# One PSUM operand in the vector operations of norms, reciprocal roots and activations of a two-layer diffusion backbone

## The chip, the cores and the metric

The kernel runs on one core of a Trainium2 chip, as one launch. The metric is the device time of the core in microseconds. The engines that matter are TensorE (PE, with its weight loads as PEld), VectorE (DVE), ScalarE (ACT), GpSimd (POOL) and SyncE (SP), which issues most DMAs. PSUM is the memory that TensorE writes its results to, eight banks of 512 float32 columns on 128 partitions; SBUF is the larger memory that holds everything else.

## What is computed

The reference runs two layers over 512 latent tokens (stream X) and 256 context tokens (stream C) with 1024 features. Each layer is a half-step SwiGLU feed-forward network (FFN), a token mixer (layer 0: gated convolution and Fourier mixing; layer 1: differential and latent attention) and a second FFN. Each of these parts has a norm ahead of it and a norm behind it:

```python
def rmsnorm(x, g):
    x32 = x.astype(jnp.float32)
    y = x32 * lax.rsqrt(jnp.mean(x32 * x32, axis=-1, keepdims=True) + EPS)
    return (y * g.astype(jnp.float32)).astype(x.dtype)

def modulate(h, g, shift, scale):
    return rmsnorm(h, g) * (1 + scale) + shift

def swiglu(x, w_in, w_out):
    gate, up = jnp.split(x @ w_in, 2, axis=-1)
    return (jax.nn.silu(gate) * up) @ w_out

def macaron_ffn(h, m, g, w_in, w_out, slot):
    xm = modulate(h, g[2 * slot], m[:, :, 3 * slot], m[:, :, 3 * slot + 1])
    y = swiglu(xm, w_in, w_out)
    return h + FFN_RES * m[:, :, 3 * slot + 2] * rmsnorm(y, g[2 * slot + 1])
```

The shift, scale and gate vectors `m` come from the conditioning vectors (adaLN), a product that the kernel computes on VectorE. The last norms have only X to serve, which the kernel then handles as two halves of 256 tokens, A and B.

## The kernel before

**Layout.** Features lie on partitions, tokens on columns: a stream is eight tiles `h[k]` of 128 x 512 (X) or 128 x 256 (C, A, B). Products are made to float32 accuracy in three matmuls (`mm3`, L213 to L215): each operand is split into a rounded high part and a low remainder, and high x high, high x low and low x high are added in PSUM. Weights come by SP's DMAs into `wraw`, ScalarE copies the high part `wh` (L141), and the low part `wl` is a subtraction on POOL or VectorE in turn (L142, L143). While a norm is under way (`self.norms`), all of these subtractions go to POOL.

**PSUM.** Three rings share the eight banks: `mm` has three slots of one bank, `st` one slot of one bank, `pr` two slots of two banks. The matmuls of C, and of the output projections of both streams, go to `mm`; gate and up of X to `pr`; norm statistics to `st`.

**A norm.** While the last block of an output projection runs, each finished tile is added to `y` (L486), ScalarE squares it (L235) and VectorE adds the square to `ssum` (L236). When all eight are done, PE multiplies `ssum` with ones into `st` (L249), VectorE computes the reciprocal root with some twelve operations of two or four columns (`rsqrt`, L264 to L275: a first guess by integer arithmetic and three Newton steps), and PE spreads it over the partitions (L255). Then `post` runs for each tile k: `t = y * A * rb` (L315), `h += t` (L317), square, add to `ssum`. A second L249, root and L255 follow, and `pre` makes the input of the next part: `t = h * A * rb` (L294), its high part on ScalarE (L300), its low part on VectorE (L301); for tile 0 of X, the low part is made by POOL (L298). `activated` (L413, with `split`) forms silu(gate) x up and its two parts.

**What sets the order.** One program is written out in Python; its jobs are interleaved by a clock of estimated microseconds (`advance`, `yield`), and a list scheduler then fixes the order on each engine, with a higher priority for the norms. On the chip each engine runs its own list in order. X's norm is placed beside the last gate, up and output projection of C; C's norm beside the first gate and up matmuls of X's next part. Stream X is lane `x`, C lane `c`; A and B are lanes `x` and `c`. In the first FFN, X starts with `lead6`: three pairs of gate and up at once, two of them in `pr`, the third in two `mm` slots.

Of the kernel before, what the change touches and what calls it, by code (L numbers as in the profile page):

```python
# [10 lines left out]
F32 = mybir.dt.float32  # L11
# [3 lines left out]
AF = mybir.ActivationFunctionType  # L15
ALU = mybir.AluOpType
AX = mybir.AxisListType

P = 128
# [3 lines left out]
CTX = 256  # L23
FT = 2816 // P
EPS = 1e-6
# [1 line left out]
POST = (1.8, 1.1)  # L27
N1 = 3.0
N2 = 4.0
POOL_LO = (0,)  # L30
LEAD = 2
TBUFS = 3
TABUFS = 2
# [43 lines left out]
class Builder:  # L77
# [146 lines left out]
    class Stats:  # L224
        pass

    def stats_add(self, s, st, src):

        nc = self.nc
        if st.ssum is None:  # L230
            st.ssum = self.tmp.tile([P, s.n], F32, name=self.nm("ssum"), tag=f"ssum{s.lane}", bufs=1)
            nc.scalar.activation(out=st.ssum, in_=src, func=AF.Square)
        else:
            sq = self.t(s.n)
            nc.scalar.activation(out=sq, in_=src, func=AF.Square)  # L235
            nc.vector.tensor_tensor(out=st.ssum, in0=st.ssum, in1=sq, op=ALU.add)  # L236

# [5 lines left out]
    def rnorm(self, s, st, width):  # L243

        nc = self.nc
        with self.tc.high_priority(PRIORITY):
            cp = self.bank()
            for b in range(s.nb):
                nc.tensor.matmul(cp[:, b:b + 1], st.ssum[:, b * P:(b + 1) * P], self.ones, start=True, stop=True)  # L249
            r = self.rsqrt(cp[:, :s.nb], 1.0 / width)  # L250
        yield N2
        with self.tc.high_priority(PRIORITY):
            bc = self.bank()
            for b in range(s.nb):
                nc.tensor.matmul(bc[:, b * P:(b + 1) * P], r[:, b:b + 1].to_broadcast([P, P]), self.ident,  # L255
                                 start=True, stop=True)
        self.clock += s.nb * 0.213
        return bc[:, :s.n]

    def rsqrt(self, src, scale, eps=EPS):  # L260

        v, n = self.nc.vector, src.shape[-1]
        r, t, m = (self.tmp.tile([P, 8], F32, name=self.nm("rs"), tag="rs", bufs=6)[:, :n] for _ in range(3))
        if isinstance(eps, float):  # L264
            v.tensor_scalar(out=m, in0=src, scalar1=scale, scalar2=eps, op0=ALU.mult, op1=ALU.add)
        else:
            v.scalar_tensor_tensor(out=m, in0=src, scalar=scale, in1=eps, op0=ALU.mult, op1=ALU.add)
        v.tensor_scalar(out=r.bitcast(I32), in0=m.bitcast(I32), scalar1=-0.5, scalar2=float(0x5F3759DF),
                        op0=ALU.mult, op1=ALU.add)
        v.tensor_scalar(out=m, in0=m, scalar1=-0.5, scalar2=None, op0=ALU.mult)  # L270
        for _ in range(3):
            v.tensor_tensor(out=t, in0=r, in1=r, op=ALU.mult)
            v.tensor_tensor(out=t, in0=t, in1=m, op=ALU.mult)  # L273
            v.scalar_tensor_tensor(out=r, in0=t, scalar=1.5, in1=r, op0=ALU.add, op1=ALU.mult)
        return r  # L275

# [13 lines left out]
    def pre_tile(self, s, k, A, B, rb):  # L290
        nc = self.nc
        x = self.xmpool.tile([P, 2, s.n], F32R, name=self.nm("xm"), tag=f"xm{s.name}{k}", bufs=1)
        t = self.t(s.n)
        nc.vector.scalar_tensor_tensor(out=t, in0=s.h[k], scalar=A[:, k:k + 1], in1=rb, op0=ALU.mult, op1=ALU.mult)  # L294
        if s.n == 512 and k in POOL_LO:
            nc.scalar.activation(out=t, in_=t, func=AF.Identity, bias=B[:, k:k + 1])
            nc.scalar.activation(out=x[:, 0], in_=t, func=AF.Copy)
            nc.gpsimd.tensor_tensor(out=x[:, 1], in0=t, in1=x[:, 0].bitcast(F32), op=ALU.subtract)  # L298
        else:
            nc.scalar.activation(out=x[:, 0], in_=t, func=AF.Identity, bias=B[:, k:k + 1])  # L300
            nc.vector.scalar_tensor_tensor(out=x[:, 1], in0=t, scalar=B[:, k:k + 1], in1=x[:, 0].bitcast(F32),  # L301
                                           op0=ALU.add, op1=ALU.subtract)
        return x[:, 0], x[:, 1]

    def post(self, s, st, A, want_stats=True):

        nc = self.nc
        y = s.y
        yield N1
        rb = yield from self.rnorm(s, st, D)  # L310
        new = self.new_stats()
        for k in range(KT):
            with self.tc.high_priority(PRIORITY):
                t = self.t(s.n)
                nc.vector.scalar_tensor_tensor(out=t, in0=y[k], scalar=A[:, k:k + 1], in1=rb,  # L315
                                               op0=ALU.mult, op1=ALU.mult)
                nc.vector.tensor_tensor(out=s.h[k], in0=s.h[k], in1=t, op=ALU.add)  # L317
                if want_stats:
                    self.stats_add(s, new, s.h[k])
            yield POST[0] if s.n == 512 else POST[1]  # L320
        yield 2.0
        return new
# [86 lines left out]
    def activated(self, s, f, g, u, acts):  # L409
        nc = self.nc  # L410
        t = self.ffpool.tile([P, s.n], F32, name=self.nm("ta"), tag="ta", bufs=TABUFS)
        nc.scalar.activation(out=t, in_=g, func=AF.Silu)
        nc.vector.tensor_tensor(out=t, in0=t, in1=u, op=ALU.mult)  # L413
        a = self.ffpool.tile([P, 2, s.n], F32R, name=self.nm("act"), tag=f"act{s.name}", bufs=5)
        self.split(t, a[:, 0], a[:, 1])
        acts[s, f] = (a[:, 0], a[:, 1])

    def lead4(self, s, ws, lead=None):
# [51 lines left out]
    def out_proj(self, s, b, c, w, acts, stats):  # L470

        nc = self.nc
        k0, nk = BLOCKS[b]
        nm = 8 // nk
        last = b == len(BLOCKS) - 1
        if b == 0 and c == 0:
            self.new_y(s)
        for i in range(nm):
            m = c * nm + i
            ps = self.mm()[:, :s.n]  # L480
            for k in range(nk):
                self.mm3(ps, self.wk(w, i * nk + k), acts[s, k0 + k], k == 0, k == nk - 1)
            if b == 0:
                nc.scalar.activation(out=s.y[m], in_=ps, func=AF.Copy)
            else:
                nc.vector.tensor_tensor(out=s.y[m], in0=s.y[m], in1=ps, op=ALU.add)  # L486
            if last:
                self.stats_add(s, stats[s], s.y[m])

    def ffn(self, l, i, s0, s1, done, ahead=0, extra=False):  # L490

# [58 lines left out]
    def mixer(self, X, C, done):  # L550
        nc, io = self.nc, self.io
# [3 lines left out]
        stats = {X: self.new_stats(), C: self.new_stats()}  # L555
# [109 lines left out]
        def out(s, m, w):  # L665
            ps = self.mm()[:, :s.n]
            order = [4, 5, 6, 7, 0, 1, 2, 3]
            for k in order:
                self.mm3(ps, self.wk(w, k), ycat[s][k], k == order[0], k == order[-1])
            nc.vector.tensor_copy(s.y[m], ps)  # L670
            self.stats_add(s, stats[s], ps)

        for step in MIX.split():
            what, s, i = step[0], {"x": X, "c": C, "b": None}[step[1]], int(step[2:] or 0)
# [149 lines left out]
    def latents(self):  # L824
# [27 lines left out]
        def keep(s, ps, lst, st):  # L852
            if lst is cq:
                tag, bufs = (("oda", 2), ("oda", 2), ("om", 1))[len(lst)]
                t = self.stg.tile([P, s.n], F32, name=self.nm("lat"), tag=tag, bufs=bufs)
            else:
                t = pool().tile([P, s.n], F32, name=self.nm("lat"), bufs=1)
            nc.scalar.activation(out=t, in_=ps, func=AF.Copy)
            self.stats_add(s, st, ps)
            lst.append(t)  # L860

        def q_lat(*ws):
# [250 lines left out]
    def da_end(self, st, g):  # L1113

        nc = self.nc
        nc.vector.scalar_tensor_tensor(out=st.den_da, in0=st.den_da, scalar=EPS, in1=st.den_da,
                                       op0=ALU.mult, op1=ALU.mult)
        rs = self.rsqrt(st.comp, 1.0 / P, st.den_da)
        for hd in range(2):
            bc = self.bank()  # L1120
            for b in range(4):
                c = hd * 4 + b
                nc.tensor.matmul(bc[:, b * P:(b + 1) * P], rs[:, c:c + 1].to_broadcast([P, P]), self.ident,
                                 start=True, stop=True)
            o = st.o_da[hd]
            nc.vector.scalar_tensor_tensor(out=o, in0=o, scalar=self.gsub, in1=bc, op0=ALU.mult, op1=ALU.mult)
            self.keep_o(g, hd, o)
# [82 lines left out]
    def attention(self, X, C, A, B, close_xm, done):  # L1210
# [34 lines left out]
        def out2(s, ms, w):  # L1245
# [6 lines left out]
            for m in ms:  # L1252
# [4 lines left out]
                    self.mm3(ps, self.wk(w, o + k), (t[:, 0, c], t[:, 1, c]), k == 0, k == len(xs) - 1)  # L1257
                o += len(xs)
                nc.vector.tensor_tensor(out=s.y[m], in0=s.y[m], in1=ps, op=ALU.add)
                self.stats_add(s, stats[s], s.y[m])  # L1260
            if ms[-1] == KT - 1:
                done(s, stats[s])

# [41 lines left out]
def body(tc, io, stop=99):  # L1305
    nc = tc.nc
    with ExitStack() as es:
# [109 lines left out]
        def begin():  # L1417
            st.update({s: b.new_stats() for s in (X, C)})
            for k in range(KT):
                b.stats_add(X, st[X], X.h[k])  # L1420
                if k == 1:
                    b.silu_late()
            norm = b.rnorm(X, st[X], D)
# [24 lines left out]
            def first():  # L1448
# [1 line left out]
                b.adaln_open(("c_ctx",))  # L1450
                load_h(C, hc, "ctx")
                for k in range(KT):
                    b.stats_add(C, st[C], C.h[k])
                    yield F2 / 8
                rb = yield from b.rnorm(C, st[C], D)
                C.xm = []
# [171 lines left out]
```

## Time and profile before

| what | value |
|---|---|
| time, median of 3 runs | 3148.69 us (3148.49 to 3149.75) |
| time of the profiled execution | 3151.14 us |
| span of the profiled execution, first to last instruction | 3149.4 us |
| mean granted clock of TensorE | 0.964 of full speed |
| ScalarE and POOL busy | 1061.5 us and 829.8 us |
| sums of squares on VectorE (L236), 172 additions | 167.4 us |
| memory read and written | 374.09 MB and 35.00 MB |

The span is cut in stretches by what runs in it: the start up to 190 us, an FFN's inner part at 190 to 560 us, the change from the first FFN to the mixer at 560 to 760 us, and so on. A group of the profile is all instructions of one line and one shape; it has their busy time, the mean length of one, and the idle time of the engine before them with what ended it. An instruction that has started but can't go on counts as busy.

### The profile page before, as it was taken

The page shows a single profiled execution, that of the slowest core. Times are in us where ns is not written, and L with a number is a line of the kernel's source. Part 1 is how long each engine was busy: PE and PEld are TensorE (multiplying, and loading weights), DVE is VectorE, ACT ScalarE, POOL GpSimd, SP SyncE. Part 2 cuts the span into 40 slices and gives each one's busy share as a digit, 9 for nine tenths or more (in the row PEclk, how much of TensorE's full clock was granted, in tenths as well). Part 3 has the DMA queues.
Part 4 walks back from the last instruction along what each step waited for, and adds up shares of the span by engine and source line. Part 5 has one row for each costly group of instructions (what it writes and reads, how often), then busy time and mean ns, then how long its engine had stood idle before and what let it go on. Part 6 is the DMA issues. An engine that isn't in the chain of part 4 may idle for free. (4 is left out here: it accounts for less than half of the span.)

```text
span 3149.4 us, 44248 instructions
## 1 busy us (share of the span) xinstructions
PE 2934.5 (93%) x17842; PEld 2605.3 (83%) x17842; DVE 1888.3 (60%) x3022; ACT 1061.5 (34%) x1744; POOL 829.8 (26%) x443
## 2 busy tenths in 40 slices
PE   6999999889979999999799999988999989899997
PEld 4878888778877988888688888876788878789997
DVE  7966666775486444445865434478366757863336
ACT  5322122334233321223431221234354546452223
POOL 4211111322242211113321111132333332442222
PEclk9999999989989999999899999989999999899998
DMA  7743334323333422232243333332876684442233
GB/s 262 237 138 127 129 120 141 107 67 122 107 119 121 135 82 99 93 108 96 79 140 114 121 116 118 114 127 96 259 186 179 156 206 96 144 154 93 96 107 122
DMA packets 189807, 412.14 MB, mean 131 GB/s; under 512 B 58337, under 2 KB 83553, under 8 KB 189602
## 3 DMA queue, kind: packets, MB, share of 16 engines
q1 hardware_dynamic: 126642, 372.05, 35.2%
q0 software_dynamic: 62960, 37.27, 5.7%
q8 instruction: 140, 2.29, 0.3%
q14 instruction: 65, 0.53, 0.1%
HBM read 374.09 MB, written 35.00 MB: 130 GB/s over the span
## 5 line engine op out<-in xcount | busy, mean ns | idle before, releaser
L143 POOL TENSOR_TENSOR wl<-wraw,wh 128x1024 fp32r<-128x1024 f32 (+1 forms) x274 | 676.9, 2473 | 2013.8 <-ACT wh L141 1992.1
L141 ACT ACTIVATE wh<-wraw 128x1024 fp32r<-128x1024 f32 (+2 forms) x474 | 491.0, 1037 | 981.2 <-PE mm L214 657.3
L213 PE MATMUL mm<-xm,wh 128*128 128x256 f32 (+1 forms) x1992 | 592.6, 298 | 10.9 <-ACT t L235 5.0
L215 PE MATMUL mm<-xm,wl 128*128 128x256 f32 (+1 forms) x1992 | 591.8, 297 | 0.3 <-DVE wl L143 0.3
L214 PE MATMUL mm<-xm,wh 128*128 128x256 f32 (+1 forms) x1992 | 591.2, 297 | 0.8 <-DVE xm L301 0.8
L214 PE MATMUL pr<-xm,wh 128*128 128x512 f32 (+1 forms) x1328 | 511.7, 385 | 7.8 <-POOL xm L1442 3.6
L213 PE MATMUL pr<-xm,wh 128*128 128x512 f32 (+1 forms) x1328 | 509.5, 385 | 7.4 <-ACT xm L300 4.0
L215 PE MATMUL pr<-xm,wl 128*128 128x512 f32 (+1 forms) x1328 | 510.7, 385 | 1.8 <-POOL wl L143 1.8
L213 PE MATMUL mm<-act,wh 128*128 128x256 f32 (+1 forms) x1408 | 464.7, 331 | 42.1 <-DVE ta L413 32.3
L214 PE MATMUL mm<-act,wh 128*128 128x256 f32 (+1 forms) x1408 | 464.4, 330 | 2.4 <-DVE act L221 2.2
L215 PE MATMUL mm<-act,wl 128*128 128x256 f32 (+1 forms) x1408 | 464.1, 330 | 0.2 <-DVE wl L143 0.2
L213 PEld LDWEIGHTS mm<-xm,wh 128*128 128x128 f32 x1992 | 381.6, 192 | 23.8 <-ACT t L235 5.4
L214 PEld LDWEIGHTS mm<-xm,wh 128*128 128x128 f32 x1992 | 381.2, 191 | 11.3 <-DVE xm L301 1.6
L215 PEld LDWEIGHTS mm<-xm,wl 128*128 128x128 f32 x1992 | 381.2, 191 | 9.7 <-DVE wl L143 0.5
L362 DVE CUSTOM_DVE_ANT_0 junk<-wmod,cond 128x1024 bf16<-128x1024 f32 x256 | 372.4, 1455 | 4.1 <-DMA wmod<-in_w_mod_dram 2.0
L143 DVE TENSOR_TENSOR wl<-wraw,wh 128x1024 fp32r<-128x1024 f32 x200 | 251.0, 1255 | 195.1 <-ACT wh L141 194.5
L213 PEld LDWEIGHTS mm<-act,wh 128*128 128x128 f32 x1408 | 272.6, 194 | 71.3 <-DVE ta L413 34.9
L214 PEld LDWEIGHTS pr<-xm,wh 128*128 128x128 f32 x1328 | 255.6, 193 | 60.9 <-POOL xm L1442 5.8
L213 PEld LDWEIGHTS pr<-xm,wh 128*128 128x128 f32 x1328 | 254.8, 192 | 58.0 <-ACT xm L300 4.4
L215 PEld LDWEIGHTS pr<-xm,wl 128*128 128x128 f32 x1328 | 255.3, 192 | 53.6 <-POOL wl L143 2.4
L214 PEld LDWEIGHTS mm<-act,wh 128*128 128x128 f32 x1408 | 273.1, 194 | 29.1 <-DVE act L221 4.8
L215 PEld LDWEIGHTS mm<-act,wl 128*128 128x128 f32 x1408 | 273.1, 194 | 25.1 <-DVE wl L143 0.7
(235 smaller groups left out, 3775.0 us busy)
## 6 DMA issues: line engine op xcount, KB each, us to landing
wraw<-in_w_ffn_in_dram SPq DMA_DIRECT2D x250, 512.0 KB, 3.5
wmod<-in_w_mod_dram SPq DMA_DIRECT2D x160, 512.0 KB, 3.8
wraw<-in_w_ffn_out_dram SPq DMA_DIRECT2D x104, 512.0 KB, 3.5
dr<-stg SPq DMA_DIRECT2D x40, 512.0 KB, 3.9
wraw<-in_w_in_even_dram SPq DMA_DIRECT2D x32, 512.0 KB, 3.5
qs<-dr POOLq DMA_DIRECT2D x56, 256.0 KB, 11.8
dr<-stg SPq DMA_DIRECT2D x36, 256.0 KB, 6.9
ks<-dr POOLq DMA_DIRECT2D x24, 384.0 KB, 11.2
```

The lines of the kernel that those rows point to most:

```text
L141: self.nc.scalar.activation(out=h, in_=r, func=AF.Copy)
L143: eng.tensor_tensor(out=l, in0=r, in1=h.bitcast(F32), op=ALU.subtract)
L213: mmul(out, w[0], x[0], start=first, stop=False)
L214: mmul(out, w[0], x[1], start=False, stop=False)
L215: mmul(out, w[1], x[0], start=False, stop=last)
L362: dot = nc.vector.tensor_tensor_reduce(out=junk, in0=w, in1=self.cond[n], op0=ALU.mult, op1=ALU.add, scale=1.0, scalar=0.0, accum_out=par[ ...
```

## The change

Each vector operation of the norms, the roots and the activations that had two operands in SBUF gets one of them in PSUM:

- The scratch tile `t` of `post` and `pre`, and the tile that receives a square, come from `scratch`: for lane `c` a slot of `mm`, for lane `x` halves of a `pr` slot. In the output projections, the mixer's output, the latents of the attention and its output projection, the square overwrites the matmul's own result tile `ps`. In the opening (`begin`, `first`), the squares go to `mm` slots.
- `rsqrt` holds `m` and `t` in columns 8 and 16 on of the `st` bank from which it reads; its Newton step multiplies r by m and then by r, where it squared r first. The attention's subnorm takes an `st` bank for it.
- `activated` multiplies in place in PSUM, and the split reads from there.
- `POOL_LO` is gone: tile 0 of X is handled like the others.

The core of the diff (the other sites of `stats_add` pass `ps`, as in `out_proj`):

```diff
-POOL_LO = (0,)
...
-    def stats_add(self, s, st, src):
+    def scratch(self, s, k, keep=False):
+
+
+        if s.lane == "c":
+            return self.mm()[:, :s.n]
+        if k == 0 or k % 2 == 0 and not keep:
+            s.scr = self.pr()
+        return s.scr[:, k % 2 * 512:k % 2 * 512 + s.n]
+
+    def stats_add(self, s, st, src, sq):
...
-            sq = self.t(s.n)
...
-            r = self.rsqrt(cp[:, :s.nb], 1.0 / width)
+            r = self.rsqrt(cp[:, :s.nb], 1.0 / width, cp)
...
-    def rsqrt(self, src, scale, eps=EPS):
+    def rsqrt(self, src, scale, bank, eps=EPS):
...
-        r, t, m = (self.tmp.tile([P, 8], F32, name=self.nm("rs"), tag="rs", bufs=6)[:, :n] for _ in range(3))
+        r = self.tmp.tile([P, 8], F32, name=self.nm("rs"), tag="rs", bufs=3)[:, :n]
+        m, t = bank[:, 8:8 + n], bank[:, 16:16 + n]
...
-            v.tensor_tensor(out=t, in0=r, in1=r, op=ALU.mult)
-            v.tensor_tensor(out=t, in0=t, in1=m, op=ALU.mult)
+            v.tensor_tensor(out=t, in0=r, in1=m, op=ALU.mult)
+            v.tensor_tensor(out=t, in0=r, in1=t, op=ALU.mult)
...
-        t = self.t(s.n)
+        t = self.scratch(s, k, True)
...
-        if s.n == 512 and k in POOL_LO:
-            nc.scalar.activation(out=t, in_=t, func=AF.Identity, bias=B[:, k:k + 1])
-            nc.scalar.activation(out=x[:, 0], in_=t, func=AF.Copy)
-            nc.gpsimd.tensor_tensor(out=x[:, 1], in0=t, in1=x[:, 0].bitcast(F32), op=ALU.subtract)
...
-                t = self.t(s.n)
+                t = self.scratch(s, k)
...
-                    self.stats_add(s, new, s.h[k])
+                    self.stats_add(s, new, s.h[k], t)
...
-        nc.vector.tensor_tensor(out=t, in0=t, in1=u, op=ALU.mult)
+        nc.vector.tensor_tensor(out=u, in0=t, in1=u, op=ALU.mult)
...
-        self.split(t, a[:, 0], a[:, 1])
+        self.split(u, a[:, 0], a[:, 1])
...
-                self.stats_add(s, stats[s], s.y[m])
+                self.stats_add(s, stats[s], s.y[m], ps)
...
-        rs = self.rsqrt(st.comp, 1.0 / P, st.den_da)
+        rs = self.rsqrt(st.comp, 1.0 / P, self.bank(), st.den_da)
...
-                b.stats_add(X, st[X], X.h[k])
+                b.stats_add(X, st[X], X.h[k], b.mm())
...
-                    b.stats_add(C, st[C], C.h[k])
+                    b.stats_add(C, st[C], C.h[k], b.mm()[:, :CTX])
```

The scheduler gives each engine nearly the same instructions (VectorE 3018 for 3016, ScalarE 1643 for 1648, POOL 440 for 444) in an order that differs at some places.

VectorE's list in X's `post` after the first FFN, before; h_109 to h_115 are tiles of X, the operations of 256 columns belong to C's activation:

```order
637 L315 SCALAR_TENSOR_TENSOR t_4907<-y_1434,par_804,st_4902 128x512
638 L315 SCALAR_TENSOR_TENSOR t_4921<-y_1435,par_804,st_4902 128x512
639 L317 TENSOR_TENSOR h_109<-h_109,t_4907 128x512
640 L317 TENSOR_TENSOR h_111<-h_111,t_4921 128x512
641 L315 SCALAR_TENSOR_TENSOR t_4945<-y_1436,par_804,st_4902 128x512
642 L236 TENSOR_TENSOR ssum_4910<-ssum_4910,t_4924 128x512
643 L317 TENSOR_TENSOR h_113<-h_113,t_4945 128x512
644 L315 SCALAR_TENSOR_TENSOR t_4988<-y_1437,par_804,st_4902 128x512
645 L236 TENSOR_TENSOR ssum_4910<-ssum_4910,t_4948 128x512
646 L413 TENSOR_TENSOR ta_4951<-ta_4951,mm_4880 128x256
```

The same place of the changed kernel, whose lines are four to seven further on (L319 was L315, L321 was L317, L243 was L236, L417 was L413):

```order
637 L319 SCALAR_TENSOR_TENSOR pr_4896<-y_1432,par_802,st_4891 128x512
638 L321 TENSOR_TENSOR h_109<-h_109,pr_4896 128x512
639 L319 SCALAR_TENSOR_TENSOR pr_4896<-y_1433,par_802,st_4891 128x512
640 L319 SCALAR_TENSOR_TENSOR pr_4932<-y_1434,par_802,st_4891 128x512
641 L321 TENSOR_TENSOR h_111<-h_111,pr_4896 128x512
642 L321 TENSOR_TENSOR h_113<-h_113,pr_4932 128x512
643 L243 TENSOR_TENSOR ssum_4899<-ssum_4899,pr_4896 128x512
644 L417 TENSOR_TENSOR mm_4869<-ta_4937,mm_4869 128x256
645 L243 TENSOR_TENSOR ssum_4899<-ssum_4899,pr_4932 128x512
646 L319 SCALAR_TENSOR_TENSOR pr_4932<-y_1435,par_802,st_4891 128x512
```

The scratch and the square now lie in two `pr` slots, the product of the activation in an `mm` slot, and C's activation stands between X's sums a little earlier.

PE's list at X's second statistics matmul (L249) in the same norm, before; act tiles of 256 columns are C's, so the matmuls around it are C's last output projection:

```order
3107 L213 MATMUL mm_5172<-act_4954,wh_5042 128x256
3109 L213 MATMUL mm_5133<-act_5118,wh_5036 128x256
3110 L213 MATMUL mm_5149<-act_5118,wh_5036 128x256
3111 L215 MATMUL mm_5172<-act_4954,wl_5043 128x256
3112 L249 MATMUL st_5182<-ones,ssum_4910 128x1 x4
3113 L213 MATMUL mm_5172<-act_5033,wh_5042 128x256
```

And in the changed kernel (L256 was L249, L212 to L214 were L213 to L215):

```order
3130 L214 MATMUL mm_5183<-act_5016,wh_5025 128x256
3131 L212 MATMUL mm_5183<-act_5096,wh_5025 128x256
3132 L213 MATMUL mm_5183<-act_5096,wh_5025 128x256
3133 L256 MATMUL st_5159<-ones,ssum_4899 128x1 x4
3134 L214 MATMUL mm_5183<-act_5096,wl_5026 128x256
3135 L212 MATMUL mm_5205<-act_4854,wh_5099 128x256
```

It stands 23 matmuls further behind in C's output projection, at its fourth tile instead of among the first three.

PE's list in the first FFN's `lead6`, at the first xm tile of X, before; wx are the weights of the third pair:

```order
13 L213 MATMUL pr_393<-xm_215,wh_314 128x512
14 L214 MATMUL pr_393<-xm_215,wh_314 128x512
15 L215 MATMUL pr_393<-xm_215,wl_315 128x512
16 L213 MATMUL mm_394<-xm_215,wx_254 128x512
17 L214 MATMUL mm_394<-xm_215,wx_254 128x512
18 L215 MATMUL mm_394<-xm_215,wx_255 128x512
```

And in the changed kernel, where xm_238 is the second tile:

```order
13 L212 MATMUL pr_392<-xm_214,wh_313 128x512
15 L212 MATMUL pr_391<-xm_238,wh_221 128x512
16 L214 MATMUL pr_392<-xm_214,wl_314 128x512
17 L213 MATMUL pr_391<-xm_238,wh_221 128x512
18 L214 MATMUL pr_391<-xm_238,wl_222 128x512
19 L212 MATMUL pr_391<-xm_238,wh_245 128x512
```

The six matmuls per tile of the third pair, 48 in all, no longer stand between the tiles: they follow behind the last of them, since the `mm` slots are given to the squares of the opening first.

More of the change, by code (lines that the diff above doesn't have):

```diff
@@ L292, in pre_tile @@
         x = self.xmpool.tile([P, 2, s.n], F32R, name=self.nm("xm"), tag=f"xm{s.name}{k}", bufs=1)
-        t = self.t(s.n)
+        t = self.scratch(s, k, True)
         nc.vector.scalar_tensor_tensor(out=t, in0=s.h[k], scalar=A[:, k:k + 1], in1=rb, op0=ALU.mult, op1=ALU.mult)
-        if s.n == 512 and k in POOL_LO:
-            nc.scalar.activation(out=t, in_=t, func=AF.Identity, bias=B[:, k:k + 1])
-            nc.scalar.activation(out=x[:, 0], in_=t, func=AF.Copy)
-            nc.gpsimd.tensor_tensor(out=x[:, 1], in0=t, in1=x[:, 0].bitcast(F32), op=ALU.subtract)
[L299 to L302, printed above, removed]
+        nc.scalar.activation(out=x[:, 0], in_=t, func=AF.Identity, bias=B[:, k:k + 1])
+        nc.vector.scalar_tensor_tensor(out=x[:, 1], in0=t, scalar=B[:, k:k + 1], in1=x[:, 0].bitcast(F32),
+                                       op0=ALU.add, op1=ALU.subtract)
         return x[:, 0], x[:, 1]
@@ L670, in out @@
             nc.vector.tensor_copy(s.y[m], ps)
-            self.stats_add(s, stats[s], ps)
+            self.stats_add(s, stats[s], ps, ps)
         for step in MIX.split():
@@ L858, in keep @@
             nc.scalar.activation(out=t, in_=ps, func=AF.Copy)
-            self.stats_add(s, st, ps)
+            self.stats_add(s, st, ps, ps)
             lst.append(t)
@@ L1259, in out2 @@
                 nc.vector.tensor_tensor(out=s.y[m], in0=s.y[m], in1=ps, op=ALU.add)
-                self.stats_add(s, stats[s], s.y[m])
+                self.stats_add(s, stats[s], s.y[m], ps)
             if ms[-1] == KT - 1:
```

## The prediction

> **What bounds the kernel now.** I read the busy shares first, then TensorE's (PE's) waits, then the span in stretches, then VectorE's (DVE's) groups by shape.
>
> ```profile
> PE 2934.5 (93%) x17842; PEld 2605.3 (83%) x17842; DVE 1888.3 (60%) x3022; ACT 1061.5 (34%) x1744; POOL 829.8 (26%) x443
> ```
>
> PE is busy for 93% of the span and nothing else comes near. So a DVE saving counts only where PE stands still for DVE. The waits of PE (microseconds in all, times, longest) name those places:
>
> ```profile
> PE st L249 <- DVE ssum L236: 43.7, 15, 7.5
> PE st L255 <- DVE rs L274: 33.4, 14, 4.3
> PE mm L213 <- DVE ta L413: 32.3, 7, 6.5
> PE mm L213 <- ACT act L220: 9.5, 3, 4.4
> ```
>
> The first two are the norm chain itself: sum of squares, matmul with ones (L249), reciprocal root, broadcast (L255). The third, 32.3 us, is the activation of the other stream, queued on DVE behind the same chain. The stretches (length; PE, PEld, DVE, ACT, POOL busy; granted clock; DMA) say where this is:
>
> ```profile
> 190.00:560.00 370.00, 370.00 (x2063) 320.37 (x2062) 234.09 (x341) 75.78 (x101) 64.50 (x23) 1.00 0.37 126
> 560.00:660.00 100.00, 83.28 (x481) 73.81 (x480) 77.31 (x110) 39.81 (x61) 36.06 (x15) 0.90 0.29 98
> ...
> 3080.00:3149.40 69.40, 51.73 (x394) 49.90 (x393) 47.96 (x102) 22.08 (x39) 17.46 (x7) 0.87 0.36 115
> sum 904.40, PE 757.22 PEld 675.42 DVE 672.40 ACT 358.30 POOL 310.09; mean PE 68.84 PEld 61.40 DVE 61.13 ACT 32.57 POOL 28.19
> ```
>
> Inside an FFN (190 to 560 us) PE is 100% busy at clock 1.00: no DVE saving shows there. Around the norms there are eleven stretches, the first and the last shown, with their sum: 904.4 - 757.2 = **147 us of idle PE**. Their clocks are mostly 0.86 to 0.91; at 0.90 a tenth of the work is lost again, so 0.1 x 757 = some **75 us** at reduced clock. These two sums are all there is to win.
>
> **What the change removes.** DVE's groups by shape (busy us, mean ns of one | idle before):
>
> ```profile
> L236 DVE TENSOR_TENSOR ssum<-ssum,t 128x512 f32<-128x512 f32 x66 | 84.6, 1282 | 29.6 <-ACT t L235 28.0
> L486 DVE TENSOR_TENSOR y<-y,mm 128x256 f32<-128x256 f32 x200 | 83.5, 420 | 108.8 <-PE mm L215 107.7
> L236 DVE TENSOR_TENSOR ssum<-ssum,t 128x256 f32<-128x256 f32 x106 | 82.8, 782 | 25.9 <-ACT t L235 24.1
> L486 DVE TENSOR_TENSOR y<-y,mm 128x512 f32<-128x512 f32 x120 | 82.2, 685 | 86.7 <-PE mm L215 85.8
> L317 DVE TENSOR_TENSOR h<-h,t 128x512 f32<-128x512 f32 x32 | 43.2, 1357 | 0.0
> L317 DVE TENSOR_TENSOR h<-h,t 128x256 f32<-128x256 f32 x64 | 41.0, 656 | 0.0
> L301 DVE SCALAR_TENSOR_TENSOR xm<-t,par,xm 128x256 fp32r<-128x256 f32 x56 | 33.4, 638 | 2.3 <-ACT xm L300 2.1
> L315 DVE SCALAR_TENSOR_TENSOR t<-y,par,st 128x256 f32<-128x256 f32 x64 | 29.3, 473 | 8.1 <-PE st L255 7.9
> L301 DVE SCALAR_TENSOR_TENSOR xm<-t,par,xm 128x512 fp32r<-128x512 f32 x28 | 24.7, 910 | 0.5 <-ACT xm L300 0.4
> L315 DVE SCALAR_TENSOR_TENSOR t<-y,par,st 128x512 f32<-128x512 f32 x32 | 23.4, 739 | 3.6 <-PE st L255 3.6
> L272 DVE TENSOR_TENSOR rs<-rs 128x4 f32<-128x4 f32 x33 | 22.4, 678 | 0.6
> L273 DVE TENSOR_TENSOR rs<-rs,rs 128x2 f32<-128x2 f32 x48 | 15.6, 325 | 1.4
> L270 DVE TENSOR_SCALAR rs<-rs 128x2 f32<-128x2 f32 x16 | 11.4, 713 | 0.5
> L273 DVE TENSOR_TENSOR rs<-rs,rs 128x4 f32<-128x4 f32 x33 | 11.0, 335 | 0.8
> L270 DVE TENSOR_SCALAR rs<-rs 128x4 f32<-128x4 f32 x11 | 1.9, 169 | 0.3
> L265 DVE TENSOR_SCALAR rs<-st 128x4 f32<-128x4 f32 x11 | 1.8, 162 | 16.9 <-PE st L249 16.9
> ```
>
> The same addition of 512 columns takes 1282 or 1357 ns with both operands in SBUF (L236, L317) and 685 with one in PSUM (L486); at 256 columns 782 or 656 against 420. L301 and L315 show it for the three-operand form. The timeline (start, length) shows what the surplus is:
>
> ```profile
> 594.44 0.16 DVE L274 SCALAR_TENSOR_TENSOR rs<-rs,rs 128x4 f32<-128x4 f32 x1
> 594.64 2.36 DVE L272 TENSOR_TENSOR rs<-rs 128x4 f32<-128x4 f32 x1
> 597.03 0.16 DVE L273 TENSOR_TENSOR rs<-rs,rs 128x4 f32<-128x4 f32 x1
> ```
> ```profile
> 594.60 2.38 POOL L143 TENSOR_TENSOR wl<-wraw,wh 128x1024 fp32r<-128x1024 f32 x1 [3.13 <-ACT wh L141]
> 597.72 2.34 POOL L143 TENSOR_TENSOR wl<-wraw,wh 128x1024 fp32r<-128x1024 f32 x1 [0.74 <-ACT wh L141]
> ```
>
> A four-column operation of 0.16 us lasts 2.36 us, exactly as long as GpSimd's (POOL's) weight split. It stands still while POOL works, and during norms all splits are on POOL. An operation with one PSUM operand does not: L486, L315 and L265 are steady.
>
> At the steady prices the change saves: sums of squares 66 x (1282 - 685) + 106 x (782 - 420) = 77.8 us; residual adds 32 x (1357 - 685) + 64 x (656 - 420) = 36.6; L301 28 x (910 - 739) + 56 x (638 - 473) = 14.0; roots, at 160 ns each, 33 x 518 + 33 x 175 + 48 x 165 + 16 x 553 ns = 39.6. Together **168 us of DVE time**. The activation's split (L221 to one PSUM operand) is sped up too, but most of it lies in the stretches where PE is full: I count nothing. Should that cover go, it is a further gain.
>
> **What no row shows** is a write to PSUM by ScalarE (172 squares) or by DVE (96 post and 88 pre tiles, some 220 steps of roots). The nearest rows are reads:
>
> ```profile
> L235 ACT ACTIVATE t<-h 128x512 f32<-128x512 f32 x35 | 21.8, 627 | 52.3 <-DVE h L317 46.8 <-DVE zp L650 3.3 <-DMA h<-in_x_dram 1.9
> L235 ACT ACTIVATE t<-mm 128x512 f32<-128x512 f32 x10 | 5.8, 590 | 0.0
> ```
>
> ScalarE reads PSUM in 37 ns less than SBUF, DVE in 7 less (L265 against L270). So a write may cost or save 172 x 37 = 6 us on ScalarE and at most 404 x 37 = 15 on DVE. I take nothing, the value of DVE's own row, and keep both ends; ScalarE is busy for 358 of 904 us and has cover. Four lo tiles of X move from POOL to DVE: 4 x 0.74 = 3 us, of which PE needs only each first tile early: nothing.
>
> **How much of it is on the path.** Of the 172 adds to ssum, 88 belong to squares of y or of a matmul result and run while PE still computes the other tiles of that projection; only the last waits. I take out 88/172 of 77.8 = 40 and keep **128 us** on the chains.
>
> What one boundary returns: X's norm between 560 and 660 us. Its post has 8 x (1357 - 685) + 7 x (1282 - 685) = 9.6 us of surplus, two roots (17.1 + 5.8)/11 = 2.1 each, the pre's seven L301 1.2: 15 us, against 16.7 us of idle PE there. After that, C's last gate, up and projection on PE, which X's chain is hidden behind, ends about when the chain does. Late next are two things. The order puts X's second statistics matmul behind 23 more matmuls of C, at the 370/2063 = 0.18 us of the full stretch 4 us at most. And scratch tiles share three `mm` slots with C's matmuls. So 11 of 15 there. In the C norms the shapes are smaller, the scratch is `mm`, and their idle per stretch is less, so I take half. X's share of 0.73 counted twice and C's 0.5 once are 0.65, and 0.65 x 128 = **83 us** (bounds: none of it, since a static order can keep each wait, and 128).
>
> At the start something is lost:
>
> ```profile
> 70.04 0.39 PE L213 MATMUL mm<-xm,wx 128*128 128x512 f32 x1
> 70.27 0.39 PE L214 MATMUL mm<-xm,wx 128*128 128x512 f32 x1
> 75.83 0.98 PE L249 MATMUL st<-ones,ssum 128*128 128x1 f32 x4 [4.93 <-DVE par L369]
> 75.00:190.00 115.00, 101.75 (x566) 88.63 (x567) 95.41 (x163) 41.01 (x66) 27.25 (x11) 0.89 0.66 223
> ```
>
> The first FFN's six-output lead now runs its third pair, 48 matmuls, after all xm tiles instead of between them. At 0.23 us each, from start to start, that is 11 us, of which PE would have had to do only the last tile's 1.4: 10 later, 5 of them in the wait of 4.93. The rest falls into the 13 us of idle PE in 75 to 190, with DVE at 95 of 115 us. Between 0 and 5 lost, and I take 2.
>
> Sum: 83 - 2 = 81. The profiled execution took 3151.1 us (its span is 3149.4), so 3070; it stands 2.4 above the median of the runs, 3148.7, which gives **3068**.
>
> [...]
>
> **Rivals.**
> - *Most waits stay* (0.13). The order on each engine is fixed when the program is built, and C's additions stand between X's in DVE's queue; the chain is shorter but its neighbours are late. A quarter of 128 returns: 3116. For: PE's third wait is for the other stream. Against: DVE is 672/904 = 74% busy in the stretches, so what is shorter moves its whole queue.
> - *The clock comes back too* (0.07).
>
> ```profile
> 620.00:630.00 10.00, 2.44 (x12) 1.94 (x12) 9.54 (x11) 3.78 (x7) 5.12 (x2) 0.62 0.36 141
> 630.00:640.00 10.00, 9.75 (x47) 9.75 (x48) 6.40 (x18) 3.93 (x7) 2.67 (x2) 0.52 0.03 8
> ```
>
> PE idles for 7.6 of 10 us, then works at 0.52. If the gaps fall below the length that does this, half of the 75 us follows: 3148.7 - 81 - 37 = 3030, with three quarters 3012. [...] Against: gaps shrink, few vanish.
> - *Slots run out; slower* (0.08). 96 scratch tiles of C and B and 14 of the opening now take an `mm` slot, and 88 matmul tiles keep theirs through square and add. All stand in the ring of three that PE needs. A post tile lives 473 + 420 + 413 + 420 ns = 1.7 us, a kept one 0.8 longer:
>
> ```profile
> L235 ACT ACTIVATE t<-y 128x256 f32<-128x256 f32 x49 | 19.6, 413 | 41.1 <-DVE y L486 22.7 <-DVE y L1259 10.9 <-DVE xm L301 3.1
> ```
>
> If PE waited half of these lives, it would lose (96 x 1.7 + 88 x 0.8)/2 = 117: 3148.7 - 81 + 117 = 3185. It decides from 81/198 = 0.41 us of wait per tile. Against: a projection tile at 12 matmuls of 0.18 us is made in 2.2 us, so three slots cover 6.5.
> - *Not what it says* (0.04): an operation with one PSUM operand still stands still behind POOL, or steadier DVE only stretches POOL's splits. Time unchanged, 3149. Against: the 320 steady L486 rows.
>
> **Chances.** My forecast, gain of 50 to 128, has 0.68. The range runs from 3014, clock and all, to 3116, a quarter of the gain. About 0.2%, 6 us, is what a measurement of this kernel can tell from no change. Faster: 0.68 + 0.07 + 0.13 = 0.88; within it 0.04; slower 0.08.
>
> **What would show it.** L236, L317 and L301 at 685, 420, 739 and 473 ns; every operation of a root near 160; waits of L249 and L255 cut by half; idle PE in the eleven stretches near 65 us. Wrong would be: the same groups still above 1 us, new waits of PE for `mm` scratch of DVE or ScalarE over 40 us in all, or a shorter DVE with the same idle PE.

## The result and the profile after

| | before | changed |
|---|---|---|
| median | 3148.59 us (3143.49 to 3149.75, 4 runs) | 3045.94 us (3025.55 to 3050.77, 4 runs) |
| profiled execution | 3151.14 us, span 3149.4 | 3044.23 us, span 3042.4 |
| mean granted clock | 0.964 | 0.984 |

The ratio is 0.9665, 95% interval 0.9619 to 0.971: 103 us faster between the medians. The forecast was 3068, a gain of 81, in a range from 3014 to 3116.

The page of the changed kernel, busy time of each engine:

```profile
PE 2895.1 (95%) x17842; PEld 2559.9 (84%) x17842; DVE 1652.7 (54%) x3026; ACT 1049.8 (35%) x1740; POOL 812.8 (27%) x439
```

Two differences split the gain of the profiled executions. PE's idle time was 3149.4 - 2934.5 = 214.9 us and is 3042.4 - 2895.1 = 147.3: **68 us**. Its busy time fell by 2934.5 - 2895.1 = **39 us** for the same 17842 matmuls; as the stretches below show, it is the clock. DVE lost 1888.3 - 1652.7 = 236 us of busy time, more than twice what the kernel gained.

PE's waits, in the changed kernel (microseconds in all, times, longest):

```profile
PE mm L212 <- ACT y L488: 11.6, 15, 2.4
PE st L256 <- DVE ssum L243: 11.0, 4, 6.6
PE mm L212 <- DVE ssum L243: 10.1, 6, 8.0
...
PE mm L212 <- DVE xm L305: 9.0, 1, 9.0
...
PE st L262 <- DVE rs L283: 7.2, 2, 4.8
```

The wait for the sum of squares fell from 43.7 to 11.0, that for the root from 33.4 to 7.2, and the wait of the output projection for `ta` left the head of the list. Three waits of matmuls into `mm` (first, third and fourth line, 31 us in all) are new or grew.

The same eleven stretches of work as before, cut where the same number of matmuls has run (columns as in the prediction); the first two, the eighth, which is the attention's beginning, and the sum:

```profile
556.80:641.30 84.50, 79.20 (x481) 66.89 (x479) 54.06 (x110) 38.06 (x60) 33.49 (x14) 1.00 0.35 115
641.30:728.80 87.50, 81.13 (x479) 71.45 (x478) 51.06 (x119) 36.02 (x64) 23.40 (x13) 0.98 0.30 96
...
2047.00:2172.50 125.50, 107.26 (x559) 89.48 (x558) 67.38 (x170) 46.82 (x89) 37.73 (x23) 0.92 0.42 147
...
sum 790.30, PE 717.18 PEld 630.46 DVE 504.98 ACT 352.14 POOL 298.81; mean PE 65.20 PEld 57.31 DVE 45.91 ACT 32.01 POOL 27.16
```

The worked stretch went from 100.0 to 84.5 us and from clock 0.90 to 1.00. In the sum, PE's idle time is 790.3 - 717.2 = 73 us, where it was 147, and PE's busy time for nearly the same matmuls is 40 us less. Busy time multiplied by the granted clock, added up over all eleven rows, is 687 us before and 694 now: at full clock the work is the same, so the 40 us are the clock. The eighth goes the other way, from 115 us at clock 0.99 to 125.5 at 0.92; before it was

```profile
2145.00:2260.00 115.00, 105.53 (x559) 87.84 (x558) 74.57 (x168) 44.40 (x84) 36.99 (x21) 0.99 0.45 155
```

The last FFN, whose activations of A and B now stay in `mm`, goes the other way too: 285 us before, 300 now, for the same matmuls (first line before):

```profile
2795.10:3080.10 285.00, 284.78 (x2440) 284.46 (x2439) 113.49 (x161) 92.85 (x142) 71.81 (x30) 1.00 0.33 112
```
```profile
2681.60:2981.50 299.90, 292.86 (x2439) 290.18 (x2438) 91.34 (x160) 91.95 (x142) 71.15 (x30) 0.98 0.32 107
```

DVE's groups by shape (busy us, mean ns of one | idle before):

```profile
L243 DVE TENSOR_TENSOR ssum<-ssum,mm 128x256 f32<-128x256 f32 x99 | 41.5, 419 | 13.9 <-ACT mm L242 11.2 <-DVE ssum L243 0.5
L243 DVE TENSOR_TENSOR ssum<-ssum,mm 128x512 f32<-128x512 f32 x38 | 26.1, 686 | 33.2 <-ACT mm L242 32.8
L321 DVE TENSOR_TENSOR h<-h,pr 128x512 f32<-128x512 f32 x32 | 21.5, 682 | 0.1
L305 DVE SCALAR_TENSOR_TENSOR xm<-mm,par,xm 128x256 fp32r<-128x256 f32 x48 | 21.0, 478 | 1.8 <-ACT xm L304 1.8
L319 DVE SCALAR_TENSOR_TENSOR mm<-y,par,st 128x256 f32<-128x256 f32 x48 | 21.7, 487 | 3.6 <-PE st L262 2.5 <-ACT ssum L240 1.1
L282 DVE TENSOR_TENSOR st<-rs,st 128x4 f32<-128x4 f32 x33 | 5.4, 165 | 0.9
```

Each of those that the forecast priced stands within a few nanoseconds of its steady price: 419 for 420, 686 and 682 for 685, 478 for 473, 165 for 160. The write to PSUM costs L319 about 14 ns (487 now, 473 when it wrote to SBUF).

### The profile page after: what moved, and what is told of

It is laid out like the page before. It is cut to its first block, busy times and chain, and to the rows that moved or that the text cites. A ratio compares the mean times of both kernels' runs of the same rounds, so it can differ in the third digit from the quotient of the medians.

```text
span 3042.4 us, 44263 instructions
## 1 busy us (share of the span) xinstructions
PE 2895.1 (95%) x17842; PEld 2559.9 (84%) x17842; DVE 1652.7 (54%) x3026; ACT 1049.8 (35%) x1740; POOL 812.8 (27%) x439
## 4 chain that ended last, share of the span: by engine, by line
PE 80%; DVE 7%; issue 4%; DMA 4%; ACT 3%; POOL 2%; SPq 0%; ACTq 0%; DVEq 0%; POOLq 0%
PE mm L212 17%; PE mm L213 16%; PE mm L214 16%; PE pr L213 9%; PE pr L214 9%; PE pr L212 9%; DVE junk L366 1%; PE pr L997 1%; ACT wh L140 1%; DMA dr<-stg 1%; PE mm L1006 1%; DVE wl L142 1%; POOL wl L142 1%; DVE xm L305 1%; DMA ot<-dr 1%
## 5 line engine op out<-in xcount | busy, mean ns | idle before, releaser
L142 POOL TENSOR_TENSOR wl<-wraw,wh 128x1024 fp32r<-128x1024 f32 (+1 forms) x274 | 666.3, 2435 | 1966.4 <-ACT wh L140 1928.2
L212 PE MATMUL mm<-xm,wh 128*128 128x256 f32 (+1 forms) x1992 | 588.3, 297 | 22.9 <-DVE xm L305 9.0
L214 PE MATMUL mm<-xm,wl 128*128 128x256 f32 (+1 forms) x1992 | 589.5, 296 | 9.4 <-DVE wl L142 9.4
L213 PE MATMUL mm<-xm,wh 128*128 128x256 f32 (+1 forms) x1992 | 588.6, 295 | 0.0
L213 PE MATMUL pr<-xm,wh 128*128 128x512 f32 (+1 forms) x1328 | 510.2, 384 | 17.3 <-POOL xm L1446 9.6
L212 PE MATMUL pr<-xm,wh 128*128 128x512 f32 (+1 forms) x1328 | 507.8, 383 | 14.8 <-ACT xm L304 7.7
L214 PE MATMUL pr<-xm,wl 128*128 128x512 f32 (+1 forms) x1328 | 506.4, 381 | 3.7 <-POOL wl L142 3.7
L212 PE MATMUL mm<-act,wh 128*128 128x256 f32 (+1 forms) x1408 | 459.2, 327 | 17.0 <-ACT y L488 11.6
L213 PE MATMUL mm<-act,wh 128*128 128x256 f32 (+1 forms) x1408 | 457.3, 325 | 0.2
L214 PE MATMUL mm<-act,wl 128*128 128x256 f32 (+1 forms) x1408 | 456.9, 325 | 0.0
L212 PEld LDWEIGHTS mm<-xm,wh 128*128 128x128 f32 x1992 | 377.5, 190 | 36.4 <-DVE xm L305 9.5
L214 PEld LDWEIGHTS mm<-xm,wl 128*128 128x128 f32 x1992 | 377.3, 189 | 18.9 <-DVE wl L142 10.0
L213 PEld LDWEIGHTS mm<-xm,wh 128*128 128x128 f32 x1992 | 379.3, 190 | 11.1 <-DVE xm L305 2.1
L213 PEld LDWEIGHTS pr<-xm,wh 128*128 128x128 f32 x1328 | 252.3, 190 | 76.0 <-DVE xm L305 15.7
L212 PEld LDWEIGHTS pr<-xm,wh 128*128 128x128 f32 x1328 | 252.4, 190 | 71.7 <-ACT xm L304 15.8
L212 PEld LDWEIGHTS mm<-act,wh 128*128 128x128 f32 x1408 | 266.4, 190 | 48.4 <-ACT y L488 17.2
L214 PEld LDWEIGHTS pr<-xm,wl 128*128 128x128 f32 x1328 | 252.5, 190 | 53.9 <-POOL wl L142 4.1
L213 PEld LDWEIGHTS mm<-act,wh 128*128 128x128 f32 x1408 | 268.9, 191 | 25.4 <-DVE act L220 1.7
L214 PEld LDWEIGHTS mm<-act,wl 128*128 128x128 f32 x1408 | 266.8, 189 | 23.5
```

Of the source, the lines that this page charges most:

```text
L142: eng.tensor_tensor(out=l, in0=r, in1=h.bitcast(F32), op=ALU.subtract)
L212: mmul(out, w[0], x[0], start=first, stop=False)
L213: mmul(out, w[0], x[1], start=False, stop=False)
L214: mmul(out, w[1], x[0], start=False, stop=last)
```

## The experiments

Ratios are to the kernel before, on the same chip; where a ratio's interval leaves out 1, the difference is clear of noise.

| kernel | median us | ratio (95%) |
|---|---|---|
| root_only | 3106.61 | 0.987 (0.9848 to 0.9892) |
| scratch_only | 3061.35 | 0.9726 (0.9712 to 0.9741) |
| act_only | 3153.85 | 1.0022 (1.0009 to 1.0035) |
| no_pool_in_norms | 3062.18 | 0.9729 (0.9715 to 0.9744) |
| act_in_sbuf | 3030.18 | 0.9619 (0.9605 to 0.9634) |
| act_sbuf_ab | 3027.02 | 0.9612 (0.9599 to 0.9626) |
| act_sbuf_ab_again | 3025.19 | 0.9616 (0.9603 to 0.9629) |
| att_sbuf_c | 3031.08 | 0.9629 (0.961 to 0.9649) |
| lead_squares_sbuf | 3045.56 | 0.967 (0.9657 to 0.9683) |
| after_again (the change once more) | 3035.56 | 0.9647 (0.9631 to 0.9662) |
| after_no_pool | 3082.04 | 0.9794 (0.9781 to 0.9808) |
| combo | 3026.18 | 0.9612 (0.9591 to 0.9632) |

### One part of the change at a time

**root_only** is the kernel before with the diff of `rsqrt` alone.

> The kernel before with only the reciprocal roots changed (m and t in the st bank). Theory (surplus on the norm chain returns, with part of the clock): the roots are 40 of the 128 us of surplus on the chains, and the whole change returned about 103 us, so 25 to 37 us here: 3112 to 3124. L281, L282 steps of four columns near 160 ns, the adds to ssum unchanged at about 1280 ns. Rival (a root is waited for behind other work of DVE anyway): under 10 us, 3140 or more.

It gave 41 us, a little over the upper end. Eight of them stand in the last FFN, between the norms: it took 277.0 us where that of the kernel before took 285.0, at clock 1.00 and with next to no waits in both, because this build's matmuls of 256 columns follow each other faster (444 per 50 us, where the kernel before has 431; see the last section). That leaves 33, inside the range. The steps cost 164 ns, and the adds to `ssum` stayed slow:

```profile
L236 DVE TENSOR_TENSOR ssum<-ssum,t 128x512 f32<-128x512 f32 x66 | 83.0, 1258 | 29.3 <-ACT t L235 27.7
L274 DVE TENSOR_TENSOR st<-rs,st 128x4 f32<-128x4 f32 x33 | 5.4, 164 | 0.9
```

**scratch_only** leaves `rsqrt` and `activated` as they were and takes the rest of the diff.

> The kernel before with only the scratch tiles and squares in PSUM, and tile 0 of X handled like the others; roots and activation as before. Theory: 88 of 128 us of surplus, so about 70 us: 3070 to 3090, with the new waits of the changed kernel for mm slots in the attention's projections (8 and 9 us) and in the opening. Rival (slots eat most of it): over 3110.

It gave 87 us, more than expected, with the two waits in the attention (8.5 and 8.1 us).

**act_only** is the product and split of `activated` in PSUM.

```diff
-        nc.vector.tensor_tensor(out=t, in0=t, in1=u, op=ALU.mult)
+        nc.vector.tensor_tensor(out=u, in0=t, in1=u, op=ALU.mult)
...
-        self.split(t, a[:, 0], a[:, 1])
+        self.split(u, a[:, 0], a[:, 1])
```

> The kernel before with only the activation's product and split in PSUM. The forecast counted nothing: 3143 to 3155. Rival 1 (C's activation at a norm is itself waited for, 32 us under the wait for ta): 3120 to 3135. Rival 2 (gate and up of A and B hold their mm slot longer, which the last FFN shows as 15 us): 3155 to 3165 with new waits of PE for ACT's copy to y between 2795 and 3080 us.

It was slower by 0.2%, 0.1 to 0.35%, which is within the first expectation. It took 66 us of busy time from DVE (1822.2 for 1888.3) and returned none of it. The output projection's wait for the other stream's activation, 32.3 us for `ta` and 9.5 for ACT's `act` before, is still there for the most part, 31.2 us, now all put down to ACT; so faster splits of the activation hardly shorten it (first line). And the last FFN has the new wait of the second rival (second line):

```profile
PE mm L213 <- ACT act L220: 31.2, 7, 7.6
```
```profile
PE mm L213 <- ACT y L484: 7.0, 12, 1.4
```

The three parts sum to 41 + 87 - 6 = 122 us; together they gave 103 and, in a second series, 112. They almost add up, and better still without the 8 us of root_only's last FFN.

### What the two-SBUF operations stand still for

```diff
-                eng = self.nc.gpsimd if self.norms or j % 2 else self.nc.vector
+                eng = self.nc.gpsimd if j % 2 and not self.norms else self.nc.vector
```

> The kernel before, but while a norm is under way all weight splits go to VectorE instead of POOL; nothing in PSUM is changed. Theory (two-SBUF operations stand still behind POOL): the groups ssum<-ssum,t fall to near 690 and 420 ns and the four-column steps of the root to 160, without any operand moved; some 70 more splits of 1.25 us lie on VectorE, so the time falls by less, 0 to 40 us: 3108 to 3148. Rival (two SBUF operands are slow by themselves): the groups stay near 1280 and 780 ns and the time rises by 50 us or more.

The cause is confirmed, and the size was far off: 86 us, with no operand moved.

```profile
L236 DVE TENSOR_TENSOR ssum<-ssum,t 128x512 f32<-128x512 f32 x66 | 63.6, 964 | 27.5 <-ACT t L235 27.2
L317 DVE TENSOR_TENSOR h<-h,t 128x512 f32<-128x512 f32 x32 | 21.9, 685 | 0.1
L272 DVE TENSOR_TENSOR rs<-rs 128x4 f32<-128x4 f32 x33 | 7.4, 225 | 0.5
L143 DVE TENSOR_TENSOR wl<-wraw,wh 128x1024 fp32r<-128x1024 f32 x261 | 325.0, 1245 | 186.7 <-ACT wh L141 185.6 <-ACT t L235 0.3
```

L317 went to 685 ns and the root's step from 678 to 225 without touching PSUM. L236 only went to 964, because this mean mixes two durations: 55 of its 66 additions take 0.68 to 0.69 us, and ten of the other eleven, each beside one of the splits that POOL still has, 2.42 to 2.51. By the code, these run in a last output projection before the norm has begun.

The same count in the kernel before leaves no room for slow operands as such: of the 66 additions, the 26 that run beside an operation of POOL take 2191 ns on average and the 40 others 691. With one operand in PSUM (L486), nine run beside POOL and take 688 ns, 111 do not and take 685. In the changed kernel, 34 of L243's additions run beside POOL, at 687 ns, and 32 do not, at 685.

The 72 splits that came to DVE cost it 90 us, and the kernel still gained 86, so most of them can't lie on the chain.

**after_no_pool** makes the same edit in the changed kernel.

> The changed kernel, with all weight splits of a norm on VectorE as in no_pool_in_norms. Theory (both edits remove the same stall, and with one operand in PSUM nothing on the norm chain stands still behind POOL): they don't add; VectorE gets some 70 splits of 1.25 us, part of them on the chains: 3046 to 3075. Rival (POOL harms the chain in another way too, or the splits wait on POOL): the 86 us of no_pool_in_norms come on top in part: below 3030.

It is slower than the changed kernel by 46 us (3082.04 against 3035.56 in the same series), even more than expected. So the two edits take away one and the same stall, and once it is gone POOL's help is worth having. (The loss is larger than it looks: the last FFN of this build took 291.6 us for 299.9, at a faster pace of the matmuls, 443 per 50 us for 427, and with the same waits.) Read against no_pool_in_norms (0.9729), its 0.9794 also says what the change costs where there is little stall left to remove: some 20 us. The longest waits that it adds are in the attention's beginning:

```profile
PE mm L212 <- DVE xm L305: 10.1, 1, 10.1
PE mm L212 <- DVE ssum L243: 7.1, 1, 7.1
```

### What the change lost again

**act_in_sbuf** undoes the activation, **act_sbuf_ab** undoes it only where A and B need it:

```diff
+        v = t if s.name in "ab" else u
-        nc.vector.tensor_tensor(out=u, in0=t, in1=u, op=ALU.mult)
+        nc.vector.tensor_tensor(out=v, in0=t, in1=u, op=ALU.mult)
...
-        self.split(u, a[:, 0], a[:, 1])
+        self.split(v, a[:, 0], a[:, 1])
```

> The changed kernel with the activation's product and split back in SBUF (roots and scratch stay in PSUM). Theory (the activation in PSUM gives nothing and holds mm slots): the parts alone gave 41 and 86 us, so 3016 to 3035, and the last FFN has no waits for ACT's copy to y. Rival (the activation's gain only shows once DVE is fast; parts overlap): 3046 or more.

> The changed kernel with the activation in SBUF for A and B alone (last FFN). Theory: the last FFN's 7.0 us of waits and half of its 10.2 us at half clock go, 12 us: 3030 to 3038. Rival (those waits come from somewhere else): 3043 to 3050, waits there unchanged.

act_in_sbuf came out in its range, act_sbuf_ab 3 us faster than its own. The median of act_sbuf_ab is 9 to 19 us below the two of the changed kernel. Its interval (up to 0.9626) and that of its repetition (up to 0.9629) lie below that of after_again (from 0.9631), but both overlap the wide one of the changed kernel's first series (from 0.9619); act_in_sbuf overlaps both, and it is not the faster of the two. So as far as these runs tell, what the activation costs, it costs in the last FFN. There the waits are gone, 7.0 us in the changed kernel and 0.2 here (second line):

```profile
PE mm L212 <- ACT y L488: 7.0, 12, 1.4
```
```profile
PE mm L212 <- ACT y L489: 0.2, 1, 0.2
```

But that part of the work shrank from 300 to 278 us, by more than the waits and the clock can give. The rest is the pace of the matmuls in a stretch of 50 us in which PE never waits, at clock 1.00 (second line act_sbuf_ab):

```profile
2850.00:2900.00 50.00, 50.00 (x427) 50.00 (x426) 16.88 (x31) 13.84 (x21) 9.61 (x4) 1.00 0.29 98
```
```profile
2850.00:2900.00 50.00, 50.00 (x443) 50.00 (x442) 19.39 (x31) 13.23 (x19) 11.99 (x5) 1.00 0.32 100
```

That is 50 us / 427 = 117 ns and 50 / 443 = 113 ns per matmul, over 2439 matmuls some 10 us. I ran act_sbuf_ab a second time for it:

> act_sbuf_ab once more. In its first trace the matmuls of 256 columns in the last FFN came every 113.3 ns, in the changed kernel's two traces every 117.8; over some 2450 matmuls that is 11 of the 19 us. Theory (the pace belongs to the program as built): 113.3 again, 3023 to 3030. Rival (the pace is that of one load of a program): 116 to 118 ns and 3032 to 3040, so that only the waits, some 8 us, belong to the edit.

443 to 444 matmuls per 50 us came back, and 3025 us: the pace belongs to the program as built, for these two programs in two traces each. What in the program sets it stays open. It isn't the activation: root_only has 444 and after_no_pool, with the activation in PSUM, 443, while combo below, with the activation of A and B in SBUF, has 427. So of the 22 us, some 13 belong to the edit, waits and clock: combo's last FFN, without waits and at the changed kernel's pace, took 286.8 us.

**att_sbuf_c** gives C's `post` and `pre` SBUF scratch from `attn_begin` until the C latents:

```diff
-            return self.mm()[:, :s.n]
+            return self.t(s.n) if self.sbuf_c else self.mm()[:, :s.n]
```

> The changed kernel with C's scratch of post and pre in SBUF from the begin of the attention to its C latents. Theory (the two waits of 8.0 and 9.0 us are mm slots that C's scratch holds): both waits and most of the 20 us at half clock after them go, 15 to 25 us: 3021 to 3031. Rival (the slots are held by X's latents, or C's chain becomes slow behind POOL): 3040 to 3050 with a wait of 5 us or more left there.

The 9.0 us wait went, but one of 6.6 for the squares of X's latents stayed, and C's now slower chain (its sums of squares there take 952 ns instead of 419) added 4.3:

```profile
PE mm L213 <- DVE ssum L244: 6.6, 1, 6.6
PE st L257 <- DVE t L320: 4.3, 1, 4.3
```

Its median is 4 to 15 us below that of the changed kernel, but the intervals of the ratios overlap (0.961 to 0.9649 against 0.9631 to 0.9662): not settled.

**lead_squares_sbuf** puts the squares of the opening into SBUF, which brings the third pair of `lead6` back between the xm tiles:

```diff
-                b.stats_add(X, st[X], X.h[k], b.mm())
+                b.stats_add(X, st[X], X.h[k], b.t(SEQ))
...
-                    b.stats_add(C, st[C], C.h[k], b.mm()[:, :CTX])
+                    b.stats_add(C, st[C], C.h[k], b.t(CTX))
```

> The changed kernel with the squares of the opening (X and C) in SBUF, by which the third pair of lead6 stands between the xm tiles again. Theory (the forecast's 0 to 5 us): 3041 to 3046, the stretch to 75 us about 5 us shorter. Rival (VectorE bounds the opening anyway): no change, 3046; or the later wait for the DVE weight split of 8.4 us stays and eats it.

No clear gain: 3045.6, where the changed kernel had 3045.9 and 3035.6. The opening and what follows it, in this kernel and in the changed one:

```profile
0.00:73.90 73.90, 46.50 (x164) 34.01 (x164) 59.94 (x102) 38.28 (x59) 32.33 (x22) 0.95 0.77 263
73.90:186.00 112.10, 97.65 (x566) 86.06 (x567) 91.07 (x161) 40.75 (x66) 27.84 (x10) 0.91 0.67 226
```
```profile
0.00:80.70 80.70, 48.19 (x165) 34.39 (x166) 64.22 (x119) 39.29 (x61) 32.49 (x22) 0.94 0.74 258
80.70:186.70 106.00, 96.87 (x567) 85.46 (x566) 85.04 (x143) 39.50 (x64) 26.13 (x10) 0.95 0.66 226
```

The 7 us won up to there are lost by 186 us, where both arrive: PE then waits 4.9 us for `par` and 6.2 for the split of an activation, where the changed kernel has the third pair to do.

**after_again and combo** ran in one series. Combo joins act_sbuf_ab, lead_squares_sbuf and att_sbuf_c, and puts the squares of the latents into SBUF.

> The changed kernel once more, beside the kernel before on the same chip as the two below. 3038 to 3050, since its four runs so far lie between 3026 and 3051.

> The changed kernel with the activation of A and B in SBUF, the squares of the opening in SBUF, and in the attention's beginning C's scratch and the squares of the latents in SBUF. Theory (each of these mm waits is a loss of its own): 19 from the activation of A and B, 0 to 5 from the opening, 10 to 20 from the attention: 3002 to 3020, no wait of PE for an mm slot over 4 us left between the FFN of layer 1 and the attention. Rival (the waits only move on): 3025 or more.

after_again came out at 3036, faster than its range: the changed kernel's time differs more between series than its first four runs told. Combo is faster than the kernel before, and 9 us faster than after_again with intervals that overlap a little (0.9591 to 0.9632 against 0.9631 to 0.9662), but at 3026 no faster than act_sbuf_ab alone: the expectation missed. The 17 us of waits in the attention's beginning became 5.1 for a square and 3.3 for a vector operation. Its last FFN runs at the slow pace of 427, 9 us longer than in act_sbuf_ab (286.8 against 277.9), so it gained about as much elsewhere; the total alone can't tell the edits to the ring from the pace.

## Why the prediction was right, and where its sizes were off

- **What bounds the kernel, and the mechanism.** Right. DVE's surplus in the norms was time standing still behind POOL's splits; no_pool_in_norms shows it without PSUM, root_only and scratch_only show it with, and so does each operation's length with and without POOL beside it.
- **Steady prices: 168 us.** Right to a few per cent, from L486, L315 and L265 of the trace before: the groups that were counted save 164 us in the changed kernel's trace, and the root's steps that were not (L274, L268) some 13 more. An operand in PSUM costs the root's steps next to nothing: at two columns they take 165 ns with one (L282), and the steady step without one took 158 before (L272).
- **0.65 x 128 = 83 us on the path.** The eleven stretches lost 147 - 73 = 74 us of idle time, 9 less than forecast. In the attention's beginning, idle time rose from 9 to 18 us: there the share of a half was wrong in sign. C's scratch holds `mm` slots (att_sbuf_c took that wait away), and the squares of X's latents hold others. No term named that place.
- **Clock: nothing in the forecast, 39 us in the result.** This is the step that was mis-sized most. It stood as a rival with a chance of 0.07 and a price of half of 75 us, and that price came out nearly exact: PE's busy time fell by 39. The closeness is luck, since no row stood behind the half. It was argued against with "gaps shrink, few vanish". Most did vanish: the waits of the two norm matmuls on `ssum` and the root went from 29 to 6. In the worked stretch PE's longest waits before, and all of them in the changed kernel (second part), are

```profile
PE mm L213 <- DVE ta L413: 6.5, 1, 6.5
PE st L255 <- DVE rs L274: 4.2, 2, 2.3
PE mm L213 <- ACT act L220: 3.3, 1, 3.3
```
```profile
PE pr L213 <- DVE xm L305: 2.0, 7, 0.3
PE pr L212 <- ACT xm L304: 1.6, 1, 1.6
PE mm L212 <- ACT act L219: 1.0, 1, 1.0
```

  none over 1.6 us where 6.5 was the longest, and its clock is 1.00. The measured 3046 lies midway between the forecast, 3068, and that rival, 3030: idle time came out 9 us short, the last FFN lost 15, and the clock, counted at nothing, made up for both and more. The rival supposes a length of gap below which the clock stays full; that is the author's estimate, and no run gives such a length. This stretch fits it: waits up to 1.6 us, clock 1.00. The last FFN does not: no wait of PE there is over 1.4 us, and yet from 2720.7 to 2731.0 us, amid waits of 0.5 to 1.4 us about every 2, the clock is 0.50. So the longest gap alone does not decide it, and no run varied the length of a gap by itself.
- **The activation at nothing.** Nearly. By itself it costs 0.2%. In the changed kernel, it adds 7 us of waits in the last FFN and loses some 5 at the lower clock (10.3 us at 0.50), where A and B both have their gate and up in `mm`; the forecast looked only at DVE's cover there and not at how long the slot is kept.
- **The opening: 2 us.** Zero. The 4.9 us wait for `par` was there in the kernel before and is back in lead_squares_sbuf; the changed kernel fills it with the third pair. It reaches 732 matmuls at 186.7 us, where the kernel before had 730 at 190.
- **Slots run out.** The mechanism is there, the price isn't: the three `mm` waits listed above come to 31 us for 198 tiles, 0.16 us each, where 0.41 would have made the change worthless. 24 of the 31 us stand in two stages, the attention's beginning and the last FFN.
- **Most waits stay; not what it says.** Both refuted, by the waits that fell and by the steady groups.

## To carry to other kernels

When an operation's mean duration is well above the same operation's elsewhere, look for what runs beside it on another engine and price it from the row where nothing does; then decide which of the two engines is to give way, since here one line that moved POOL's work gave 86 us, and moving the operands 103 to 112. When a chain with many waits gets shorter, price the clock with the idle time: here 74 us less of idle time in the norms came with 40 us less of busy time at the same work. Short waits in a row came with a lower clock too: 12 waits of PE up to 1.4 us in the last FFN, and 10.3 us at clock 0.50, where the kernel before, with 0.2 us of waits, had 1.00. Scratch in PSUM is paid for in the ring that it takes its slots from, here with 24 us of waits for `mm` in two stages, so look at the stage where all users of that ring meet.

## Not expected

The pace of matmuls of 256 columns at full clock was not one number: per 50 us in the last FFN it was 431 before and in scratch_only and act_only, 426 or 427 in five builds (the changed kernel in both of its traces among them) and 443 or 444 in four others, one of them traced twice. It is a difference of 4%, some 10 us here, as large as most effects that were tested, and it follows no edit that I could name. Whoever compares two builds by their totals compares this as well.

The changed kernel's own runs spread over 25 us (3025.55 to 3050.77), those of act_sbuf_ab over 6 (3023.6 to 3029.24 and 3022.72 to 3027.38). What the difference is, no trace here shows.
